# A fused hybrid decoder layer in fp32: the scores move ahead of the values in each block's run

## The chip, the cores and the metric

One core of one Trainium2 chip runs the whole kernel. The metric is device time in microseconds (us): the median of three runs. The profiler records one execution, from which the span and every duration below come.

## The reference, cut to what matters

One layer of a hybrid decoder over 4096 prompt tokens and 64 sample tokens, width 1024. All of it is float32.

```python
h = rmsnorm(x, g_pre);  z = h @ w_in          # columns: conv group, q, k, v, gates, memory q, memory gate
out_a = silu(cg) * cb * conv3(cc * ch)        # 256 channels
out_b = silu(ag) * window_attention(q, k, v)  # window 128, 8 q heads on 2 kv heads, head 64, one sink logit per head
out_c = silu(mg) * memory_attention(mq, mk, mv)   # 4 heads, 256 memory tokens
y = concat(out_a, out_b, out_c) @ w_out
x + rmsnorm(y, g_post)
```

The window attention is computed for blocks of 128 queries against 256 keys (their own block and the one before). The outputs are y for prompt and sample tokens, and the new key, value and convolution states.

## The kernel before, in words

**Two parts.** `input_projection` computes z for all tokens in three phases and leaves queries, keys, values and the gates (`mix`, group outputs that are still without attention) in memory. It ends at about 950 us. The attention part follows: 31 prompt blocks of 128 tokens, then the 64 sample tokens, then the last prompt block. The change is in the attention part alone.

**A block of the attention part.** `Block.run` multiplies the mixed operand of block b by `w_out`. The product has two halves of 512 columns, `y_0` (p = 0) and `y_1` (p = 1), each of 24 matmuls: 8 steps k of three, because fp32 is split into a rounded high part and a rest (`mh`, `ml` of the operand, and two parts of the weights). `y_0` accumulates in PSUM bank 0, `y_1` in bank 5. Each half is multiplied by the gain (DVE, `yn`) and squared and summed in place (ACT, L1466). Then DVE and POOL make the norm factor (`yst`), and DVE adds the residual (`xr`, L1476).

**The work of other blocks between the matmuls.** `events_of(i)` hangs work onto places (p, k) of block i. At (0, 0) stands `values_and_scores(i)`, at (1, 0) `transposes(i)`, at (1, 3) the split of the next block's operand (`Block.split`: ACT casts the high part `mh`, DVE subtracts for `ml`), and loads stand at others. Work on one group of 128 queries is spread over four blocks: its scores in block g - 3, the transposes of the probabilities in block g - 2, the values in block g - 1, and the output product in block g.

**The run.** `values_and_scores` issues the small matmuls that use part of the PE array (`tiled`: half the rows or half the columns at a time). They are called a block's run here. Before the change it holds, in this order: 16 matmuls of the memory values (`cross_values`, tile `pv`), then on DVE the memory gate (L1218), 16 matmuls of the window values into the same `pv`, on DVE the window gate (L1250), 12 window scores into banks 0 and 1 (`ws`), 12 memory scores into banks 4 and 5 (`xs`), and 12 window scores into banks 2 and 3. ACT copies each window score bank (L1141), and DVE puts the other half of the keys in by a predicated copy from the bank (L1142), which frees it. Softmax follows: for the memory `xmx`, `xnm`, `xp`, `xrd`, and for the window `wmx`, `wnm`, `wes`, eight exponentials on `sm` (L1153), `wden`, `wrd` and the scaling of `sm` (L1156).

**Banks.** Tags of the pool `psb` are banks 0 to 5; `pv` is a tile of two banks of its own. Bank 0 is used by `ws_0` in the run and by `y_0` after it. Bank 5 is used by `y_1` and then by `xs_1` in the next run. The transposes use banks 1 to 4.

**What sets the order.** On each engine instructions are executed in order. The order is chosen by a scheduler from dependencies and priorities at build time; `tc.keep_in_program_order(ins)` pins an instruction to its place in the program. Inside a run all tiled matmuls but the first are pinned (`run_open`). The cast `mh` is not pinned before the change. In the built program it stands on ACT directly behind the square of `y_1` and ahead of the four copies of scores, and `ml` stands on DVE ahead of the four predicated copies.

Of the kernel before, what the change touches and what calls it, by code (L numbers as in the profile page):

```python
# [15 lines left out]
P = 128  # L16
# [9 lines left out]
CT = 256  # L26
NCH = 4096 // CT
# [24 lines left out]
def hybrid_layer(ctx: ExitStack, tc: tile.TileContext, a: dict):  # L52
# [927 lines left out]
    chunks = {}  # L980

    def open_attention():
# [5 lines left out]

        ps = {tag: ctx.enter_context(tc.tile_pool(name=f"ps{tag}", bufs=1, space=bass.MemoryType.PSUM)) for tag in ("b", "pv")}
        vp = ctx.enter_context(tc.tile_pool(name="vp", bufs=5, side="right"))  # L990
# [40 lines left out]
    class Chunk:  # L1031
# [38 lines left out]
        def values(self, vt_prev, pv=None):  # L1070

            self.vts = [vt_prev]
            ts = [psum(0, f"vtp{self.c}_{i}")[:, 0:P] if pv is None else pv[:, 1, 256 + P * i : 256 + P * i + P] for i in range(2)]
            for i in range(2):
# [9 lines left out]
    class Group:  # L1084
# [24 lines left out]
        def scores(self):  # L1109
            self.open_scores(0)  # L1110
            self.open_scores(3)
            bands = [psum(n, f"ws{self.b}_{n}").rearrange("p (h k) -> p h k", h=2) for n in range(4)]
            cross = [psum(4 + hh, f"xs{self.b}_{hh}").rearrange("p (j k) -> p j k", j=2) for hh in range(2)]
            self.bands(bands[:2], 0)
            self.crosses(cross)
            self.bands(bands[2:], 1)
            self.band_softmax()

# [92 lines left out]
        def cross_values(self, o):  # L1211
            c = self.chunk
            for j in range(2):
                both_values(o[:, j * P : j * P + P], *([(third["mv"][:, kt, j * P : (j + 1) * P],
                                                         self.xpt[hh][:, CT * kt + P * j : CT * kt + P * j + P]) for kt in range(2)]
                                                       for hh in range(2)))
            g = c.mix[:, 2:4, self.i * P : self.i * P + P]
            V.tensor_tensor(g, g, o.rearrange("p (j n) -> p j n", j=2), op=ALU.mult)  # L1218

        def early_values(self, n):  # L1220
            c = self.chunk
            if n == 3:
                self.cross_values(psum(0, f"xo{self.b}")[:, :CT])
                return
# [6 lines left out]
        def values(self):  # L1231
# [11 lines left out]
            for n in range(2):  # L1243
                for kvh in range(2):
                    cs, rs = slice(64 * kvh, 64 * kvh + 64), slice(64 - 64 * n, 128 - 64 * n)
                    v, p3 = step(n, kvh)
                    tiled(o[cs, 1 - n], v[rs, cs], p3[rs, :, 64 - 64 * n : 128 - 64 * n], start=False, stop=True,
                          tile_position=(64 - 64 * n, 64 * kvh))
            g = c.mix[:, 4:8, self.i * P : self.i * P + P].rearrange("p h (a q) -> p a h q", a=2)
            V.tensor_tensor(g, g, o, op=ALU.mult)  # L1250
# [3 lines left out]
    def values_and_scores(i):  # L1254

        run_open[0] = False
        if 2 <= i + 1 < 2 * NCH:
            groups.pop(i + 1).values()
        if i + 3 < 2 * NCH:
            groups[i + 3] = Group(chunks[(i + 3) // 2], (i + 3) % 2)  # L1260
            groups[i + 3].scores()

    def transposes(i):
        g, c = i + 2, (i + 2) // 2
        if g < 2 * NCH:
            if g % 2 == 0:
                chunks[c].values(chunks[c - 1].vts[2], values_psum(f"vtp{c}"))
            groups[g].transposes()
# [148 lines left out]
    class Block:  # L1417
# [10 lines left out]
        def split(self):  # L1428
# [10 lines left out]
            hi, lo = parts(f"mh{b}"), parts(f"ml{b}")  # L1439
            S.copy(hi, src)  # L1440
            V.tensor_tensor(lo, src, f(hi), op=ALU.subtract)  # L1441
            self.hl = [hi, lo]

        def run(self, last, events):
# [6 lines left out]
            for p, (c0, c1) in enumerate(parts):  # L1451
                acc = psum((0, 5, 1)[p], f"y{b}_{p}")[:, : c1 - c0]
                j, passes = 0, 3 if m == P else 2
# [42 lines left out]
    def events_of(i):  # L1496
# [5 lines left out]

        at(0, 0, values_and_scores, i)
        if i + 2 < len(blocks):
            at(0, 0, blocks[i + 2].load)
        if i % 2 == 0:
            at(0, 1, chunk_load, i // 2 + 3)
            if i // 2 + 3 < NCH:
                at(1, 2, lambda: chunks[i // 2 + 3].load_values())
            if i == 28:  # L1510
                at(0, 1, lambda: chunks[15].load_mix())
        elif (i + 3) // 2 < NCH - 1:
            at(0, 3, lambda: chunks[(i + 3) // 2].load_mix())
        at(1, 0, transposes, i)
        if i + 1 < len(blocks) and blocks[i + 1].b != 32:
            at(1, 3, blocks[i + 1].split)
        for (n, p, k), stage in sample.items():
# [118 lines left out]
```

## Time and profile before

| | |
|---|---|
| median of 3 runs | 1606.21 us (1604.33 to 1607.09) |
| the profiled execution: time, span | 1605.98 us, 1604.3 us |
| PE busy (share of the span) | 1529.8 us (95%) |
| DVE, ACT, POOL busy | 1128.4 (70%), 777.4 (48%), 324.2 us (20%) |
| attention part, from the first score to the end | 950.9 to 1604.3 us |

The page gives busy times of each engine. Matmuls of one array shape overlap in the records, so a busy PE is not an idle-free PE: what a block costs is read from the starts of its instructions. A row of the timeline gives the start, the length, engine, line, operation, tiles and count, and in brackets the idle time of the engine before it and what ended that. PEld is the loading of weights. "The chain of waits" is the list of who waited for whom.

### The profile page before, as it was taken

The numbers are of one execution on the slowest core, as the hardware profiler recorded it, in microseconds if no ns is written. First come the engines' busy times: TensorE is split into PE (matmuls) and PEld (weight loads), VectorE is DVE, ScalarE is ACT, GpSimd is POOL, SyncE is SP. The second block draws the span as 40 slices with busy tenths as digits, with TensorE's granted clock in tenths as the row PEclk, the third lists the DMA queues.
The fourth block names the chain that finished last, engine by engine and source line by source line (L and its number), as shares of the span: only waits on it lengthen the run. The fifth ranks groups of instructions, "written<-read, shape, count | busy, mean of one in ns | idle before, by whom it ended". The sixth has DMA issues, their size and how long they took to land.

```text
span 1604.3 us, 30846 instructions
## 1 busy us (share of the span) xinstructions
PE 1529.8 (95%) x11981; PEld 1399.3 (87%) x11981; DVE 1128.4 (70%) x1850; ACT 777.4 (48%) x1964; POOL 324.2 (20%) x522
## 2 busy tenths in 40 slices
PE   9999999999999999999999998888888888888998
PEld 9999999999999999999999987777777777777776
DVE  6878888898988777976667695555555555555554
ACT  6776665565222222444435464555555555555541
POOL 0322333222100000000001022333333333333320
PEclk9999999999999999999999999999999999999999
DMA  9979999877644333798557597444444444444432
GB/s 262 213 209 264 269 274 267 277 238 187 233 167 157 121 121 131 246 294 272 190 197 243 191 303 226 132 126 130 135 131 129 125 136 131 131 130 131 143 115 92
DMA packets 169735, 299.47 MB, mean 187 GB/s; under 512 B 29813, under 2 KB 99445, under 8 KB 169557
## 3 DMA queue, kind: packets, MB, share of 16 engines
q1 hardware_dynamic: 128069, 226.69, 44.5%
q0 software_dynamic: 40800, 69.76, 16.2%
q8 instruction: 94, 1.54, 0.4%
q10 hardware_dynamic: 720, 1.05, 0.2%
q14 instruction: 52, 0.43, 0.1%
HBM read 190.38 MB, written 108.05 MB: 186 GB/s over the span
## 4 chain that ended last, share of the span: by engine, by line
PE 64%; DVE 14%; issue 8%; ACT 7%; POOL 3%; DMA 3%; SPq 0%; POOLq 0%; ACTq 0%; DVEq 0%
PE c L359 47%; PE y L1458 12%; ACT sm L1153 3%; DVE xr L1476 2%; DVE ml L1441 2%; ACT mh L1440 2%; DVE sm L1142 2%; DVE wmx L1148 1%; POOL wpt L1202 1%; DVE xmx L1161 1%; POOL yst L1472 1%; PE xt L1208 1%; PE wt L1195 1%; PE mem_acc L775 1%; ACT y L1466 1%
## 5 line engine op out<-in xcount | busy, mean ns | idle before, releaser
L1458 PE MATMUL y<-wo,mh 128*128 128x512 f32 (+1 forms) x1040 | 338.9, 396 | 42.7 <-DVE sm L1142 42.7
L1458 PEld LDWEIGHTS y<-wo,mh 128*128 128x128 f32 x1040 | 195.6, 189 | 89.8 <-DVE sm L1142 48.6
L366 DVE TENSOR_TENSOR z<-c,z 128x520 f32<-128x520 f32 (+1 forms) x308 | 195.0, 646 | 95.1 <-PE c L359 94.0
L1458 PE MATMUL y<-wo,ml 128*128 128x512 f32 (+1 forms) x520 | 202.6, 390 | 0.0
L1465 DVE TENSOR_TENSOR yn<-y,gpost 128x512 f32<-128x512 f32 (+1 forms) x66 | 45.4, 687 | 177.0 <-PE y L1458 173.5
L1458 PEld LDWEIGHTS y<-wo,ml 128*128 128x128 f32 x520 | 98.7, 190 | 17.7
L1466 ACT ACTIVATE y<-y 128x512 f32<-128x512 f32 (+1 forms) x66 | 38.0, 575 | 147.8 <-DVE yn L1465 147.8
L1168 POOL TENSOR_SCALAR xp<-xp,xrd 128x256 f32<-128x256 f32 x128 | 60.8, 486 | 224.1 <-DVE wnm L1149 122.8
L1153 ACT ACTIVATE sm<-sm,wnm 128x128 f32<-128x128 f32 x256 | 99.2, 389 | 12.9 <-DVE wnm L1149 12.9
L1164 ACT ACTIVATE xp<-xs,xnm 128x256 f32<-128x256 f32 x128 | 58.9, 473 | 66.3 <-DVE xnm L1162 66.3
L1200 POOL TENSOR_SCALAR_AFFINE_SELECT wpv<-wpt 128x512 f32<-128x512 f32 x62 | 51.8, 855 | 98.7 <-ACT wpt L1196 98.7
L1017 PEld LDWEIGHTS ws<-kst,q 64*128 64x128 f32 x768 | 50.2, 187 | 12.1 <-issue 10.8
L1017 PE MATMUL ws<-kst,q 64*128 64x256 f32 x768 | 60.0, 288 | 0.4 <-DVE z L366 0.4
L1476 DVE SCALAR_TENSOR_TENSOR xr<-yn,yst,xr 128x1024 f32<-128x1024 f32 (+2 forms) x34 | 42.5, 1253 | 22.1 <-POOL yst L1472 21.3
L1017 PE MATMUL pv<-wpv,vt 128*64 128x256 f32 (+1 forms) x240 | 39.1, 400 | 17.2 <-DVE mix L1218 8.6
L734 POOL MEMSET negs<- 128x1 f32 x1 | 0.1, 98 | 265.2 <-PE c L359 265.2
L368 ACT COPY z<-c 128x520 f32<-128x520 f32 (+1 forms) x44 | 24.4, 554 | 55.5 <-PE c L359 52.7
L1202 POOL TENSOR_SCALAR_AFFINE_SELECT wpt<-wpt 128x512 f32<-128x512 f32 x64 | 40.6, 653 | 50.7 <-ACT wpt L1196 50.4
L1142 DVE COPY_PREDICATED sm<-wmask,ws 128x256 f32<-128x256 uint8 x124 | 49.9, 441 | 0.0
L1472 POOL TENSOR_TENSOR yst<-yst,mhalf 128x1 f32<-128x1 f32 (+1 forms) x33 | 18.4, 557 | 148.0 <-DVE yst L1471 148.0
L1153 ACT ACTIVATION_READ_ACCUMULATOR sm<-sm,wnm 128x1 f32 x256 | 47.9, 187 | 0.0
L400 ACT CAST zh<-z 128x520 fp32r<-128x520 f32 x56 | 33.4, 624 | 29.2 <-DVE z L366 26.5
(957 smaller groups left out, 5027.8 us busy)
## 6 DMA issues: line engine op xcount, KB each, us to landing
q<-qd POOLq DMA_DIRECT2D x32, 768.0 KB, 8.3
xr<-in_x_p SPq DMA_DIRECT2D x32, 512.0 KB
nat<-in_x_p SPq DMA_DIRECT2D x39, 416.0 KB
o_yp<-xr SPq DMA_DIRECT2D x31, 512.0 KB
md<-th POOLq DMA_DIRECT2D x48, 260.0 KB, 6.6
qd<-zh SPq DMA_DIRECT2D x48, 260.0 KB
qd<-z SPq DMA_DIRECT2D x48, 260.0 KB
place<-md SPq DMA_DIRECT2D x8, 1024.0 KB
```

The source lines that it names most:

```text
L359: TE.matmul(bank[:, :HW], l, r, start=first and i == 0, stop=last and i == 3 * KH - 1)
L366: add = lambda dst, other: V.tensor_tensor(dst, c, other, op=ALU.add)
L1017: ins = TE.matmul(o, w, x, **kw)
L1142: V.copy_predicated(to, third["wmask"], third["negs"].unsqueeze(2).to_broadcast([P, 2, P]) if self.b == 0 else s3[:, :, 0:P])
L1153: S.activation(sm[:, h, :], sm[:, h, :], AF.Exp, bias=nm[:, h : h + 1], scale=SCALE, accum_out=den[:, h : h + 1])
L1164: S.activation(p[:, i, :], s[:, i, :], AF.Exp, bias=nm[:, i : i + 1], scale=SCALE, accum_out=den[:, i : i + 1])
L1168: G.tensor_scalar(p[:, i, :], p[:, i, :], rd[:, i : i + 1], 0.5, op0=ALU.mult, op1=ALU.mult)
L1200: G.affine_select(self.pv[u].rearrange("p (h q) -> p h q", h=4), p3, pattern=[[0, 4], [-1, P]], compare_op=ALU.is_gt, fill=0.0, base=0, ch ...
L1202: G.affine_select(p3, p3, pattern=[[0, 4], [1, P]], compare_op=ALU.is_ge, fill=0.0, base=0, channel_multiplier=-1)
L1458: TE.matmul(acc, self.hl[l][:, k], wo[k][c0 // 512][:, r, c0 % 512 : c0 % 512 + c1 - c0], start=j == 0, stop=j == passes * KT - 1)
L1466: S.activation((psum(2, "sq") if end else acc)[:m, : c1 - c0], acc[:m], AF.Square, scale=float(D) ** -0.5, accum_out=st[:m, p : p + 1])
L1476: V.scalar_tensor_tensor(self.xr[:m, cs], yn[:m, cs], st[:m, 3:4], self.xr[:m, cs], op0=ALU.mult, op1=ALU.add)
```

## The change

It reorders a block's run. The scores of group i + 3 come first, all 24 window scores before the 12 memory scores, then both values of group i + 1, and then both gates, memory and window, one behind the other (`cross_gate` is taken out of `cross_values` and called behind the window values). `band_softmax` is called after the values. The cast `mh` of blocks 1 to 30 is pinned to its place in the program, at (1, 3) of the block before. In block 0 the run is moved to (0, 3), the transposes to (1, 2) and the split to (1, 4); its two output halves use the two banks of a `pv` tile in place of banks 0 and 5, and the transposed values of chunk 1 use bank 0. The loads of values move from (1, 2) to (1, 3), and the order in which the two PSUM pools are opened is swapped.

In the built program after the change, ACT has per block: square of `y_1`, four copies of scores, two exponentials `xp` for each half, the eight of `sm`, (in every other block two copies of transposed values,) the copies of transposed probabilities with the square of `y_0` among them, and last the cast `mh`. DVE has: `yn` of `y_1`, `yst`, the predicated copy of bank 0, `xr`, the three other predicated copies, both `xmx`, `xnm`, `wmx`, `xrd`, `xnm`, `wnm`, the two gates, `xrd`, `wes`, `wden`, `wrd`, the scaling of `sm`, `yn` of `y_0`, `xpt`, and `ml`.

```diff
--- before.py
+++ after.py
@@ -986,7 +986,7 @@
         psa.close()
         pa.close()
 
-        ps = {tag: ctx.enter_context(tc.tile_pool(name=f"ps{tag}", bufs=1, space=bass.MemoryType.PSUM)) for tag in ("b", "pv")}
+        ps = {tag: ctx.enter_context(tc.tile_pool(name=f"ps{tag}", bufs=1, space=bass.MemoryType.PSUM)) for tag in ("pv", "b")}
         vp = ctx.enter_context(tc.tile_pool(name="vp", bufs=5, side="right"))
         yp = ctx.enter_context(tc.tile_pool(name="yp", bufs=2, side="right"))
         bq = att.enter_context(tc.tile_pool(name="bq", bufs=1))
@@ -1070,7 +1070,7 @@
         def values(self, vt_prev, pv=None):
 
             self.vts = [vt_prev]
-            ts = [psum(0, f"vtp{self.c}_{i}")[:, 0:P] if pv is None else pv[:, 1, 256 + P * i : 256 + P * i + P] for i in range(2)]
+            ts = [psum(0, f"vtp{self.c}_{i}")[:, 0:P] if pv is None else pv[:, P * i : P * i + P] for i in range(2)]
             for i in range(2):
                 TE.transpose(ts[i], self.vT[:, i * P : i * P + P], ident)
             for i in range(2):
@@ -1112,9 +1112,8 @@
             bands = [psum(n, f"ws{self.b}_{n}").rearrange("p (h k) -> p h k", h=2) for n in range(4)]
             cross = [psum(4 + hh, f"xs{self.b}_{hh}").rearrange("p (j k) -> p j k", j=2) for hh in range(2)]
             self.bands(bands[:2], 0)
+            self.bands(bands[2:], 1)
             self.crosses(cross)
-            self.bands(bands[2:], 1)
-            self.band_softmax()
 
         def both_rows(self, outs, q, k):
 
@@ -1214,13 +1213,17 @@
                 both_values(o[:, j * P : j * P + P], *([(third["mv"][:, kt, j * P : (j + 1) * P],
                                                          self.xpt[hh][:, CT * kt + P * j : CT * kt + P * j + P]) for kt in range(2)]
                                                        for hh in range(2)))
-            g = c.mix[:, 2:4, self.i * P : self.i * P + P]
+
+        def cross_gate(self, o):
+            g = self.chunk.mix[:, 2:4, self.i * P : self.i * P + P]
             V.tensor_tensor(g, g, o.rearrange("p (j n) -> p j n", j=2), op=ALU.mult)
 
         def early_values(self, n):
             c = self.chunk
             if n == 3:
-                self.cross_values(psum(0, f"xo{self.b}")[:, :CT])
+                o = psum(0, f"xo{self.b}")[:, :CT]
+                self.cross_values(o)
+                self.cross_gate(o)
                 return
             o = psum(0, f"wo{self.b}")
             both_values(o, *([(v, p[u]) for v, p in zip(c.vts[self.i : self.i + 2], (self.pv, self.pt)) if p[u] is not None]
@@ -1246,6 +1249,7 @@
                     v, p3 = step(n, kvh)
                     tiled(o[cs, 1 - n], v[rs, cs], p3[rs, :, 64 - 64 * n : 128 - 64 * n], start=False, stop=True,
                           tile_position=(64 - 64 * n, 64 * kvh))
+            self.cross_gate(pv[:, 0, 256 : 256 + CT])
             g = c.mix[:, 4:8, self.i * P : self.i * P + P].rearrange("p h (a q) -> p a h q", a=2)
             V.tensor_tensor(g, g, o, op=ALU.mult)
 
@@ -1253,18 +1257,21 @@
 
     def values_and_scores(i):
 
-        run_open[0] = False
+        run_open[0] = i == 0
+        g = i + 3
+        if g < 2 * NCH:
+            groups[g] = Group(chunks[g // 2], g % 2)
+            groups[g].scores()
         if 2 <= i + 1 < 2 * NCH:
             groups.pop(i + 1).values()
-        if i + 3 < 2 * NCH:
-            groups[i + 3] = Group(chunks[(i + 3) // 2], (i + 3) % 2)
-            groups[i + 3].scores()
+        if g < 2 * NCH:
+            groups[g].band_softmax()
 
     def transposes(i):
         g, c = i + 2, (i + 2) // 2
         if g < 2 * NCH:
             if g % 2 == 0:
-                chunks[c].values(chunks[c - 1].vts[2], values_psum(f"vtp{c}"))
+                chunks[c].values(chunks[c - 1].vts[2], psum(0, "vtp1")[:, :CT] if c == 1 else values_psum(f"vtp{c}")[:, 1, 256:])
             groups[g].transposes()
 
     def chunk_load(c):
@@ -1437,7 +1444,9 @@
                 return
             src = chunks[b // 2].mix[:, :, (b % 2) * P : (b % 2) * P + P]
             hi, lo = parts(f"mh{b}"), parts(f"ml{b}")
-            S.copy(hi, src)
+            copy = S.copy(hi, src)
+            if 0 < b < 31:
+                tc.keep_in_program_order(copy)
             V.tensor_tensor(lo, src, f(hi), op=ALU.subtract)
             self.hl = [hi, lo]
 
@@ -1449,7 +1458,11 @@
 
             parts = [(0, 512), (512, 768), (768, D)] if last else [(0, 512), (512, D)]
             for p, (c0, c1) in enumerate(parts):
-                acc = psum((0, 5, 1)[p], f"y{b}_{p}")[:, : c1 - c0]
+                if b == 0:
+                    both = values_psum("y0") if p == 0 else both
+                    acc = both[:, p]
+                else:
+                    acc = psum((0, 5, 1)[p], f"y{b}_{p}")[:, : c1 - c0]
                 j, passes = 0, 3 if m == P else 2
                 for k in range(KT):
                     for fn in events.get((min(p, 1), k), ()) if p < 2 else ():
@@ -1500,20 +1513,20 @@
         def at(p, k, fn, *args):
             ev.setdefault((p, k), []).append(lambda: fn(*args))
 
-        at(0, 0, values_and_scores, i)
+        at(0, 0 if i else 3, values_and_scores, i)
         if i + 2 < len(blocks):
             at(0, 0, blocks[i + 2].load)
         if i % 2 == 0:
-            at(0, 1, chunk_load, i // 2 + 3)
+            at(0, 1 if i else 4, chunk_load, i // 2 + 3)
             if i // 2 + 3 < NCH:
-                at(1, 2, lambda: chunks[i // 2 + 3].load_values())
+                at(1, 3, lambda: chunks[i // 2 + 3].load_values())
             if i == 28:
                 at(0, 1, lambda: chunks[15].load_mix())
         elif (i + 3) // 2 < NCH - 1:
             at(0, 3, lambda: chunks[(i + 3) // 2].load_mix())
-        at(1, 0, transposes, i)
+        at(1, 0 if i else 2, transposes, i)
         if i + 1 < len(blocks) and blocks[i + 1].b != 32:
-            at(1, 3, blocks[i + 1].split)
+            at(1, 3 if i else 4, blocks[i + 1].split)
         for (n, p, k), stage in sample.items():
             if n == i:
                 at(p, k, next, stage, None)
```

## The prediction

> **What bounds the kernel now.** I read the page first, for the share of the engines, then the waits of PE in the attention part, then the timeline of one pair of blocks.
>
> ```profile
> span 1604.3 us, 30846 instructions
> PE 1529.8 (95%) x11981; PEld 1399.3 (87%) x11981; DVE 1128.4 (70%) x1850; ACT 777.4 (48%) x1964; POOL 324.2 (20%) x522
> ```
>
> PE is the bound, so what counts is the time in which PE stands still. The chain of waits for PE from 956 to 1545 us has three rows (engine and tile that waited, for whom, us in total, times, longest):
>
> ```profile
> PE y L1458 <- DVE sm L1142: 42.7, 29, 3.3
> PE pv L1017 <- DVE mix L1218: 8.6, 14, 0.6
> PE pv L1017 <- DVE place L1218: 8.6, 14, 0.6
> ```
>
> There are two waits per block, in 28 blocks: one inside the run, where the window values wait for the memory gate (14 + 14 times 0.61 us), and one behind it, where `y_0` waits until bank 0 has been copied out of the scores (28 times about 1.4, and once 3.3 in block 0). The timeline of PE for one block and the next one's start:
>
> ```profile
> 1201.14 0.50 PE L1458 MATMUL y<-wo,mh 128*128 128x512 f32 x1 [1.39 <-DVE sm L1142]
> 1206.72 0.38 PE L1075 MATMUL vtp<-ident,vT 128*128 128x128 f32 x2
> 1208.60 0.47 PE L1458 MATMUL y<-wo,mh 128*128 128x512 f32 x1
> ...
> 1214.26 1.09 PE L1017 MATMUL pv<-xpt,mv 128*64 128x128 f32 x16
> 1215.97 0.65 PE L1017 MATMUL pv<-wpv,vt 128*64 128x256 f32 x4 [0.61 <-DVE mix L1218]
> ...
> 1217.58 0.98 PE L1017 MATMUL ws<-kst,q 64*128 64x256 f32 x12
> 1218.38 0.89 PE L1017 MATMUL xs<-mk,q 64*128 64x256 f32 x12
> 1219.10 0.89 PE L1017 MATMUL ws<-kst,q 64*128 64x256 f32 x12
> 1221.40 0.50 PE L1458 MATMUL y<-wo,mh 128*128 128x512 f32 x1 [1.41 <-DVE sm L1142]
> 1241.40 0.50 PE L1458 MATMUL y<-wo,mh 128*128 128x512 f32 x1 [1.39 <-DVE sm L1142]
> ```
>
> Two blocks take 1241.40 - 1201.14 = 40.26, so a block takes 20.13 us. Its run lasts from 1214.26 to 1221.40, 7.14 us. Why bank 0 comes free so late is seen on the other engines:
>
> ```profile
> 1214.37 0.69 DVE L1465 TENSOR_TENSOR yn<-y,gpost 128x512 f32<-128x512 f32 x1 [3.79 <-PE y L1458]
> 1215.15 0.58 ACT L1466 ACTIVATE y<-y 128x512 f32<-128x512 f32 x1 [4.52 <-DVE yn L1465]
> 1215.88 0.21 DVE L1471 TENSOR_SCALAR yst<-yst 128x1 f32<-128x1 f32 x1
> ...
> 1216.78 1.28 DVE L1476 SCALAR_TENSOR_TENSOR xr<-yn,yst,xr 128x1024 f32<-128x1024 f32 x1 [0.69 <-POOL yst L1472]
> 1217.98 0.68 DVE L1250 TENSOR_TENSOR mix<-mix,pv 128x512 f32<-128x512 f32 x1
> ...
> 1218.69 1.05 ACT L1440 CAST mh<-mix 128x1024 fp32r<-128x1024 f32 x1 [2.85 <-DVE mix L1250]
> ...
> 1219.65 1.19 ACT L1141 COPY sm<-ws 128x256 f32<-128x256 f32 x4
> 1219.77 1.22 DVE L1441 TENSOR_TENSOR ml<-mix,mh 128x1024 fp32r<-128x1024 f32 x1 [1.11 <-ACT mh L1440]
> 1220.92 0.77 DVE L1142 COPY_PREDICATED sm<-wmask,ws 128x256 f32<-128x256 uint8 x2
> ```
>
> It is a chain of DVE and ACT: `xr`, window gate, cast `mh`, then the copy of bank 0 behind the cast and the predicated copy behind `ml`. The scores are the last thing in the run, so nothing on PE covers it.
>
> **The run in its new order.** Its matmuls are the same, so I rebuild it from the starts above. Twelve scores take 0.80 from the first matmul to the next group (1217.58 to 1218.38) and 0.72 where the shape did not change before them (1218.38 to 1219.10); the next group of one shape thus begins 0.17 before the last one's end (1218.38 + 0.89 against 1219.10). Where the array's shape changes, the next group begins about as the last ends. So: window scores 0.80 + 0.72; memory scores 0.89, as the shape changes behind them; memory values 1.09 - 0.17 = 0.92; window values, up to the next change of shape, 1217.58 - 1215.97 = 1.61. The sum is 4.94 against 7.14: 2.20 less. There are four changes of shape before and after, so none is added. A block would take 17.93 us by PE alone.
>
> **What is late next: bank 5.** `xs_1` writes the bank of `y_1`, which is free when ACT has squared it. That is at 1215.84 (the `yst` row starts right behind it), 1.58 behind the run's start. The memory scores begin 0.80 + 0.72 = 1.52 behind it. That costs 0.1 us per block with the release, while `yn` is on time. So 18.03.
>
> **What is late next: the loop through DVE and ACT.** `ml` stands on DVE right ahead of `yn` of `y_1`, and `mh` at the end of ACT's block. A late softmax thus delays `yn`, so bank 5, so PE. The rest of the durations:
>
> ```profile
> 1201.31 1.28 DVE L1161 TENSOR_REDUCE xmx<-xs 128x2 f32<-128x512 f32 x2
> 1202.70 0.47 ACT L1164 ACTIVATE xp<-xs,xnm 128x256 f32<-128x256 f32 x1 [2.14 <-DVE xnm L1162]
> 1203.45 1.22 DVE L1148 TENSOR_REDUCE wmx<-sm 128x8 f32<-128x1024 f32 x1
> 1204.93 0.40 ACT L1153 ACTIVATE sm<-sm,wnm 128x128 f32<-128x128 f32 x1 [0.30 <-DVE wnm L1149]
> 1208.09 0.19 ACT L1153 ACTIVATION_READ_ACCUMULATOR sm<-sm,wnm 128x1 f32 x1
> 1208.75 1.23 DVE L1156 TENSOR_TENSOR sm<-sm,wrd 128x1024 f32<-128x1024 f32 x1
> 1209.10 1.05 ACT L1196 COPY wpt<-wt 128x512 f32<-128x512 f32 x2
> 1210.04 0.59 ACT L1209 COPY xpt<-xt 128x512 f32<-128x512 f32 x1
> ```
>
> From the start of `yn` (0): `yst` at 1.51, `xr` at 2.41 (1216.78 - 1214.37), its end 3.61 as the next instruction sees it (1217.98). Three predicated copies of 0.385 (0.77 for two): 4.77. Both `xmx`: 6.05. `wmx`: 7.27. The second half's exponentials can start at about 7.6, behind the small steps, and take two of 0.47: 8.5. The eight of `sm` with theirs take 1208.28 - 1204.93 = 3.35: 11.9. To the scaling 0.47 (1208.28 to 1208.75), the scaling 1.23: 13.6. `yn` of `y_0` 0.69, the square 0.6: 14.9. In every other block one copy `wpt` (0.53) comes behind the square: 15.4. `xpt` 0.59, `mh` 1.05, `ml` 1.22: 18.3, and 17.8 in the others. PE needs 18.03. So the loop and PE are nearly equal: 18.3 in one block and 18.03 in the next give 18.17 on average. I take 18.1, since each of the loop's small steps was rounded up. The two gates lie in this loop between `wnm` and `wes`, which ACT needs as its second step of the eight. They take no more than 0.68 each and end by 9.0, about when that step comes, if the values are done by 7.4; by the run above they end at 5.0. If not, what they are late is paid in the loop.
>
> The saving is 20.13 - 18.1 = 2.03 in each of 28 blocks, 56.8 us. `mh` costs nothing where it is put, since its reader comes after the next run, 5 us later.
>
> **Blocks 29 and 30** have values without scores:
>
> ```profile
> 1539.55 1.09 PE L1017 MATMUL pv<-xpt,mv 128*64 128x128 f32 x16
> ...
> 1541.47 0.65 PE L1017 MATMUL pv<-wpv,vt 128*64 128x256 f32 x4
> ```
>
> Here the window values come 1.92 behind the memory values where 0.92 would do. With the gates behind both, 1.0 goes, in two blocks 2.0. Against that, blocks 26 to 30 also carry the sample tokens' softmax on DVE and ACT, which lengthens a loop without slack: I take 1.0 back (bounds 0 and 3).
>
> **Block 0.** Here the order changes most:
>
> ```profile
> 953.49 1.23 DVE L1441 TENSOR_TENSOR ml<-place,mh 128x1024 fp32r<-128x1024 f32 x1
> 956.95 0.79 PE L1458 MATMUL y<-wo,mh 128*128 128x512 f32 x1 [3.28 <-DVE sm L1142]
> 965.12 1.04 PE L1195 MATMUL wt<-ident,sm 128*128 128x128 f32 x8
> ```
>
> ```profile
> 956.00:958.00 2.00, 1.05 (x3) 0.86 (x4) 2.00 (x5) 0.14 (x1) 0.94 (x2) 0.50 0.81 145
> 960.00:962.00 2.00, 2.00 (x6) 1.52 (x6) 1.83 (x5) 0.45 (x2) 1.48 (x4) 0.50 1.31 373
> ```
>
> `y_0` could start before the run, but its second matmul needs `ml`, which DVE ends at 954.72 behind the splits of `w_out`. So PE stands still there instead: `y_0` goes on at 954.8, 2.2 us earlier than before, but the run of 36 scores now comes into it, 2.3 to 2.5 us. The windows (PE clock is the eighth number) show that the clock granted after the gap of 3.28 us was 0.50 from 956 to 962. With a gap of about 3 us again, that stays. At half clock the run's longer stretch costs up to 3 us, at full clock the transposes come 2.2 earlier: between -2.2 and +0.8, I take -0.5. [...]
>
> The loads hang on the same queues: POOL issues `kst` and `q` right behind the scores, which now end 3 us earlier in the run, and three blocks ahead of use. I cost them at nothing; the cover is over 50 us. In block 0 they come some 8 us later, which with that cover is nothing too.
>
> **Sum.** 1605.98 - 56.8 - 2.0 + 1.0 - 0.5 = 1547.7, so **1548**. The profiled execution is 0.2 below the median, so I make no correction. A difference of 0.2% (3 us) is about what a measurement of this kernel can tell from no change.
>
> **The rivals.** (1) *The loop becomes the bound* (chance 0.22). It was computed within 0.3 of PE's need, from some 25 instructions with their handovers. If each handover costs 0.04 more, it is 1 us longer: 19.3 and 18.8, so a saving of 1.08 in 28 blocks, 30 us: 1575. In between 1557 to 1575. For it: DVE and ACT alternate without slack. Against it: the pieces are measured with their handovers. (2) *The change does not do what it says* (0.03): the predicated copy of bank 0 is still late and only the wait inside the run goes, 28 times 0.78 and 2.0: 1582. Against it: in the built order this copy stands right behind `yst`. (3) *Slower* (0.04): the exponentials no longer overlap their accumulator reads. Now the eight and one small one take 3.35 us, because the next starts 0.1 behind a read's start; without that overlap each of twelve per block costs 0.19 more, 2.3 us in the loop: 20.6 and 20.1, 20.35 on average, 0.2 over today's block: 28 times 0.2 is 6 us, 1612. It decides from a loop of 20.13 on. Against it: the rows show the overlap in the same sequence of instructions. (4) *PE alone is the bound and the start comes at full clock* (0.08): 28 times 2.2, 2.0 and 2.2: 1540.
>
> **How the numbers follow.** The forecast (0.62) spans 1542 to 1557, by 18.03 to 18.35 per block, the start, and the sample blocks. To hold 8 in 10 the range takes in half of rival 1 and some of rival 4: 1541 to 1568. Faster by over 0.2% is the forecast and rivals 1, 2 and 4: 0.95, within 0.2% 0.01, slower 0.04.
>
> **What would show it right or wrong.** In the profile after, the row of `pv` waiting for the memory gate should be gone, and that of `y` waiting for `sm` should be left in block 0 at most. A block should take 18.0 to 18.3 us. A new wait of `xs` for ACT's square of `y_1`, with 0.1 to 0.3 us, should appear. If it is 0.5 or more, rival 1 holds; its sign is `ml` ending behind the last matmul of `y_1`. If `y` still waits for `sm` by a microsecond, rival 2 does. The prediction is wrong if the blocks take over 18.8 us.

## The result, and the profile after

The changed kernel takes 1550.01 us (median of 4 runs, 1548.36 to 1553.61) against 1606.03 us (4 runs of the kernel before): a ratio of 0.9655, 95% interval 0.9635 to 0.9675. The prediction, 1548.0 with a range of 1541 to 1568, was right. The profiled execution took 1549.02 us, 56.96 less than the one before.

Three lines of the page after: the span, the engines' busy times, and the chain that ended last, which before the change began with PE 64%, DVE 14%.

```profile
span 1547.3 us, 30906 instructions
PE 1525.7 (99%) x11981; PEld 1400.8 (91%) x11981; DVE 1124.6 (73%) x1850; ACT 776.8 (50%) x1964; POOL 335.6 (22%) x522
...
PE 88%; DVE 4%; issue 3%; DMA 2%; ACT 2%; POOL 1%; SPq 0%; DVEq 0%; POOLq 0%; ACTq 0%
```

PE, DVE and ACT are busy about as long as before; PE no longer stands still. All waits of PE from 956 to 1545 us in the kernel after (for whom, us in total, times, longest):

```profile
PE y L1471 <- ACT y L1479: 3.3, 1, 3.3
PE xt L1207 <- ACT sq L1320: 0.3, 1, 0.3
```

Both waits per block are gone, and the one row of any size that is left is a single wait, in block 0 (two earlier ones of block 0 lie ahead of 956 us and are told below). The timeline of one block after, PE's rows of the run with those of DVE and ACT that release it:

```profile
1178.40 0.50 PE L1471 MATMUL y<-wo,mh 128*128 128x512 f32 x1
...
1190.15 1.23 DVE L1450 TENSOR_TENSOR ml<-place,mh 128x1024 fp32r<-128x1024 f32 x1 [2.13 <-ACT mh L1447]
...
1191.54 1.69 PE L1017 MATMUL ws<-kst,q 64*128 64x256 f32 x24
1191.64 0.69 DVE L1478 TENSOR_TENSOR yn<-y,gpost 128x512 f32<-128x512 f32 x1 [0.27 <-PE y L1471]
1192.43 0.58 ACT L1479 ACTIVATE y<-y 128x512 f32<-128x512 f32 x1 [2.31 <-DVE yn L1478]
...
1193.07 1.07 PE L1017 MATMUL xs<-mk,q 64*128 64x256 f32 x12
...
1193.41 0.45 DVE L1141 COPY_PREDICATED sm<-wmask,ws 128x256 f32<-128x256 uint8 x1
...
1194.07 1.09 PE L1017 MATMUL pv<-xpt,mv 128*64 128x128 f32 x16
1194.99 0.60 PE L1017 MATMUL pv<-wpv,vt 128*64 128x256 f32 x4
...
1196.55 0.50 PE L1471 MATMUL y<-wo,mh 128*128 128x512 f32 x1
...
1214.44 0.50 PE L1471 MATMUL y<-wo,mh 128*128 128x512 f32 x1
```

Two blocks take 1214.44 - 1178.40 = 36.04, so a block takes 18.02 us (20.13 before). The run lasts 1196.55 - 1191.54 = 5.01 us (7.14 before). The predicated copy of bank 0 ends at 1193.86, 2.7 us before `y_0` wants the bank. Before the change this copy was the last thing that `y_0` waited for.

Where the 57.0 us between the two spans come from, by the starts of the runs in both traces:

| stretch | before | after | difference |
|---|---|---|---|
| start to run 1 | 972.41 | 975.25 | +2.84 |
| run 1 to run 29 (28 blocks) | 567.14 | 508.08 | -59.06 |
| run 29 to the end | 64.75 | 63.97 | -0.78 |

The loop gave 2.11 per block, a little more than forecast, and block 0 lost what was not forecast.

### The profile page after: what moved, and what is told of

Its sections match the earlier page's. It is cut to its first block, busy times and chain, and to the rows that moved or that the text cites. A ratio compares the mean times of both kernels' runs of the same rounds, so it can differ in the third digit from the quotient of the medians.

```text
span 1547.3 us, 30906 instructions
## 1 busy us (share of the span) xinstructions
PE 1525.7 (99%) x11981; PEld 1400.8 (91%) x11981; DVE 1124.6 (73%) x1850; ACT 776.8 (50%) x1964; POOL 335.6 (22%) x522
## 4 chain that ended last, share of the span: by engine, by line
PE 88%; DVE 4%; issue 3%; DMA 2%; ACT 2%; POOL 1%; SPq 0%; DVEq 0%; POOLq 0%; ACTq 0%
PE c L359 49%; PE y L1471 24%; PE pv L1017 5%; PE ws L1017 3%; PE xt L1207 2%; PE xs L1017 2%; PE wt L1194 2%; PE mem_acc L775 1%; DMA wor<-in_w_out 1%; ACT sm L1152 1%; DMA vd<-v 1%; DVE z L366 0%; DMA wr_2A<-in_w_in 0%; DVE wo L182 0%; POOL md L163 0%
## 5 line engine op out<-in xcount | busy, mean ns | idle before, releaser
L1199 POOL TENSOR_SCALAR_AFFINE_SELECT wpv<-wpt 128x512 f32<-128x512 f32 x62 | 62.4, 1018 | 115.5 <-ACT wpt L1195 109.8
L1153 DVE TENSOR_TENSOR wden<-wden,wes 128x8 f32<-128x8 f32 x32 | 5.3, 167 | 88.3 <-ACT sm L1152 88.3
L1017 PE MATMUL ws<-kst,q 64*128 64x256 f32 x768 | 55.4, 290 | 0.0
```

The costliest lines, as they stand in the source:

```text
L1017: ins = TE.matmul(o, w, x, **kw)
L1199: G.affine_select(self.pv[u].rearrange("p (h q) -> p h q", h=4), p3, pattern=[[0, 4], [-1, P]], compare_op=ALU.is_gt, fill=0.0, base=0, ch ...
```

## The experiments

The kernel before ran beside each group of experiments, on other chips, with medians of 1607 to 1611 us. So the ratios are compared. "Block" is the mean distance between the starts of two runs over the same 21 blocks of each trace, 20.15 for the kernel before and 18.02 for the one after.

### One part of the change at a time

**The pinned cast alone**, on the kernel before:

```diff
-            S.copy(hi, src)
+            copy = S.copy(hi, src)
+            if 0 < b < 31:
+                tc.keep_in_program_order(copy)
```

> The kernel before with one part of the change alone: the cast `mh` is pinned to (1, 3) of the block before. The scores stay last in the run, the memory gate stays between the values. Theory A (the chain of DVE and ACT behind `yn` held bank 0, and the whole loop from `yn` to the next `yn` is nearly as long as a block): the wait of `y` for bank 0 goes (28 times 1.4 = 39 us, to 1567), but the scores of banks 2 and 3 now end some 5.6 us behind `yn` instead of 2.4, and the window gate stands ahead of the predicated copies, so the softmax ends about 1 us later; the loop is 18.3 + 1.0 and 17.8 + 1.0 and becomes the bound at about 19.05 a block: 1606 - 28 x 1.1 = 1575 (1567 to 1585). Rival B (only the order of the scores frees bank 0 in time): about 1606. Rival C (the loop has room): 1567, the wait for the memory gate of 0.61 stays and no other appears.

Measured: ratio 0.9755 (0.9720 to 0.9791), 1568.15 us, block 18.68. The waits of PE from 980 to 1500 us in this kernel:

```profile
PE pv L1017 <- DVE place L1218: 8.8, 14, 0.8
PE pv L1017 <- DVE mix L1218: 8.0, 13, 0.6
```

The wait for bank 0 is gone from the loop and the wait for the memory gate stays. That is rival C, 1567: the loop through DVE and ACT had room, and theory A's extra microsecond did not come. The sum of the prediction has the scaling of `sm` ahead of ACT's copies; in this timeline it lies beside them (the scaling starts at 1192.91, the copies of transposed values at 1192.94).

**The gates alone**, on the kernel before (no pin, scores last):

```diff
-            g = c.mix[:, 2:4, self.i * P : self.i * P + P]
+        def cross_gate(self, o):
+            g = self.chunk.mix[:, 2:4, self.i * P : self.i * P + P]
             V.tensor_tensor(g, g, o.rearrange("p (j n) -> p j n", j=2), op=ALU.mult)
...
+            self.cross_gate(pv[:, 0, 256 : 256 + CT])
             g = c.mix[:, 4:8, self.i * P : self.i * P + P].rearrange("p h (a q) -> p a h q", a=2)
```

> The kernel before with one part of the change alone: the memory gate stands behind the window values, ahead of the window gate; the scores stay last, the cast is not pinned. Theory A (a block before is set by one chain of DVE and ACT from the end of `y_1` over `yn`, `yst`, `xr`, window gate, `mh`, `ml` to the copy of bank 0, and the wait inside the run lies beside this chain): the wait inside the run goes and the wait of `y` grows by as much and by the memory gate's 0.35 on top, as this gate now stands on the chain: 20.13 + 0.35 a block, 1606 + 10 - 2 (blocks 29 and 30) = 1614, with a `y` wait of about 2.5 us. Rival B (the two waits add up, as a sum over waits says): 28 x 0.78 + 2 less, 1582, with a `y` wait of 1.4 us as before.

Measured: ratio 1.0196 (1.0146 to 1.0247), 1640.52 us. One of the two waits was removed, and the kernel became slower. The waits of PE from 990 to 1560 us in this kernel:

```profile
PE y L1463 <- DVE sm L1142: 71.4, 27, 2.9
```

The wait of `y` grew from 1.4 to 2.62 in most blocks, as theory A had it: the two waits lay on one chain. But blocks are of two kinds in this trace. Twelve have the expected length (20.40 and 20.64 in turn, 0.37 over the kernel before, 0.35 expected). In fifteen PE is slow after the wait and the block takes about 22.1 (two of them, which also carry work of the sample tokens, take longer). Here are two stretches of 3 us behind a wait of 2.62, with the start of `y` in each, from the same trace (in the windows the third number is PE's busy time and the eighth the granted clock):

```profile
1171.90:1174.90 3.00, 3.00 (x13) 2.46 (x14) 2.96 (x8) 1.44 (x7) 0.15 (x1) 1.00 1.20 380
1214.84:1217.84 3.00, 3.00 (x7) 2.42 (x8) 2.96 (x8) 1.43 (x7) 0.16 (x1) 0.50 1.18 359
```

```profile
1171.90 0.50 PE L1463 MATMUL y<-wo,mh 128*128 128x512 f32 x1 [2.62 <-DVE sm L1142]
...
1214.84 0.79 PE L1463 MATMUL y<-wo,mh 128*128 128x512 f32 x1 [2.62 <-DVE sm L1142]
```

At the same wait one stretch is granted 1.00 and the other 0.50. Fifteen blocks times 1.6 us, and 28 times 0.37, make 34 us, about what the ratio gives (0.0196 of 1606 is 31). Theory A was right on the chain and blind to this.

**The pin and the gates together**, scores still last, block 0 as before (both diffs above):

> The kernel before with the pinned cast and both gates behind both values; the scores stay last in the run, block 0 is as before. Theory A (the scores have to come first so that the softmax, and with it the loop through DVE and ACT, starts early): PE alone would need 17.9 a block, but both gates stand ahead of the predicated copies, so the loop is 18.3 + 1.4 and 17.8 + 1.4: about 19.4 a block, 1606 - 28 x 0.7 - 2 = 1584 (1570 to 1592). Rival B (the order of scores and values does not matter once both waits are gone): 18.0 a block and no loss in block 0, 1544 to 1550.

Measured: ratio 0.9743 (0.9711 to 0.9775), 1566.39 us, block 18.70. That is below theory A's range and far from rival B: both missed. The wait of PE in this kernel from 980 to 1500 us, and DVE's rows ahead of `y_0` in one block:

```profile
PE y L1465 <- DVE sm L1142: 21.3, 27, 1.0
```

```profile
1218.33 1.28 DVE L1483 SCALAR_TENSOR_TENSOR xr<-yn,yst,xr 128x1024 f32<-128x1024 f32 x1 [0.67 <-POOL yst L1479]
1219.53 0.41 DVE L1220 TENSOR_TENSOR mix<-mix,pv 128x256 f32<-128x256 f32 x1
...
1219.86 0.68 DVE L1255 TENSOR_TENSOR mix<-mix,pv 128x512 f32<-128x512 f32 x1
...
1220.46 0.77 DVE L1142 COPY_PREDICATED sm<-wmask,ws 128x256 f32<-128x256 uint8 x2
...
1220.94 0.50 PE L1465 MATMUL y<-wo,mh 128*128 128x512 f32 x1 [0.62 <-DVE sm L1142]
```

The wait for bank 0 is back, 21.3 / 27 = 0.79 per block, in place of the 0.62 inside the run. With the scores last, `xr` and both gates stand ahead of the copy that frees bank 0. With the cast out of the way, moving the gate only moves the wait, and the two kernels have the same block within 0.02. The last 0.68 per block (18.70 to 18.02, 19 us) needs the scores at the front of the run. What they bring with the memory gate still between the values was not run.

**The changed kernel without the pin:**

```diff
-            copy = S.copy(hi, src)
-            if 0 < b < 31:
-                tc.keep_in_program_order(copy)
+            S.copy(hi, src)
```

> The changed kernel without the pinned cast. In the built program `mh` then stands on ACT behind the eight exponentials and ahead of the copies of the transposed probabilities, and `ml` on DVE between `yn` of `y_0` and `xpt`. Theory A (bank 0 is copied out early in any case, and PE is the bound): 1548 to 1551, and the loop is shorter by up to one `ml` (1.2 us), so that `ml` no longer stands ahead of `yn`. Rival B (the copies of the transposed probabilities, 1.05 later, hold PE or the square of `y_0`): 0.5 a block or more, 1564 and over.

Measured: ratio 0.9649 (0.9617 to 0.9680), 1551.80 us, block 18.02: theory A. In the new order the pin is worth nothing that shows here. It also shows who the bound is. DVE's row at the end of a block in this kernel:

```profile
1192.28 0.69 DVE L1476 TENSOR_TENSOR yn<-y,gpost 128x512 f32<-128x512 f32 x1 [2.37 <-PE y L1469]
```

DVE now waits 2.37 us for PE ahead of `yn`, against 0.27 in the changed kernel's block above, and the block has the same length. PE is the bound.

### How near the next limits are

**The memory scores between the window scores**, in the changed kernel:

```diff
             self.bands(bands[:2], 0)
-            self.bands(bands[2:], 1)
             self.crosses(cross)
+            self.bands(bands[2:], 1)
```

> The changed kernel with the memory scores between the two halves of the window scores, in the order that they had before. Theory A (in the changed kernel the memory scores start 1.53 behind the run's start, and bank 5 is free at 1.57: the second place of 12 window scores is just the cover that the square of `y_1` needs): `xs` starts at 0.80 and waits 0.75 per block, 28 times, 21 us: 1571, with a row of `xs` waiting for ACT's square. Rival B (the wait is taken from a reserve elsewhere, as the block is bound by DVE and ACT): 1550 to 1555.

Measured: ratio 0.9803 (0.9774 to 0.9832), 1574.68 us, block 18.74, 0.72 more: theory A. From this kernel's trace, `xs` around its wait:

```profile
1195.79 0.28 PE L1017 MATMUL xs<-mk,q 64*128 64x256 f32 x1
1195.86 0.58 ACT L1479 ACTIVATE y<-y 128x512 f32<-128x512 f32 x1 [3.00 <-DVE yn L1478]
1196.60 0.98 PE L1017 MATMUL xs<-mk,q 64*128 64x256 f32 x11 [0.54 <-ACT y L1479]
```

`xs_1` goes on 0.74 behind the start of the square (1195.86 to 1196.60). With the square at 1192.43, as in the timeline of the changed kernel above, that is 1193.17, and there `xs` begins at 1193.07: bank 5 comes free just in time. Twelve more scores ahead of it are all the cover that there is.

**A longer loop**, in the changed kernel (ACT repeats one copy, so no part of the result changes):

```diff
-            (S.copy if u else V.tensor_copy)(self.xpt[u], t)
+            for _ in range(3 if u and ps is not None else 1):
+                (S.copy if u else V.tensor_copy)(self.xpt[u], t)
```

> The changed kernel, where ACT does its copy `xpt_1` of each block three times (0.59 us each, so 1.18 more, between the square of `y_0` and the cast `mh`; the same data). It lengthens the loop through ACT and DVE without touching PE. Theory A (PE is the bound, the loop lies 0.25 below it in one block and 0.47 in the next, which is the idle time of DVE ahead of `yn`): 1.18 - 0.36 = 0.82 more per block, 18.83 on average, 28 x 0.82 = 23 us: 1573, with `ml` ending behind the last matmul of `y_1` and a new wait of `xs` of about 0.8. Rival B (the loop is the bound already): 28 x 1.18 = 33 us, 1583. Rival C (ACT has room before `mh`, so the loop doesn't run through it): 1550.

Measured: ratio 0.9775 (0.9748 to 0.9802), 1571.37 us, block 18.75, 0.73 more, where 0.82 was expected: theory A. Its trace at the end of a block:

```profile
1197.56 1.84 ACT L1209 COPY xpt<-xt 128x512 f32<-128x512 f32 x3
1199.30 1.05 ACT L1448 CAST mh<-place 128x1024 fp32r<-128x1024 f32 x1
1200.38 1.23 DVE L1451 TENSOR_TENSOR ml<-place,mh 128x1024 fp32r<-128x1024 f32 x1 [3.37 <-ACT mh L1448]
...
1201.52 0.68 DVE L1479 TENSOR_TENSOR yn<-y,gpost 128x512 f32<-128x512 f32 x1
...
1202.98 0.98 PE L1017 MATMUL xs<-mk,q 64*128 64x256 f32 x11 [0.65 <-ACT y L1480]
```

This is how rival 1 of the prediction would have looked: `yn` has no idle time ahead of it, it follows `ml`, and `xs` waits 0.65. From one `yn` of `y_1` to the next this trace has 18.98 and 18.52 in turn. The three copies take 1.84, and the one in the changed kernel 0.60; without the 1.24 the loop is 17.74 and 17.28, 17.5 on average, about 0.5 under PE's 18.02.

### Block 0

Rows of block 0 in the changed kernel, from the last matmul of the input projection to the start of run 1:

```profile
948.51 0.28 PE L359 MATMUL c<-hi_7T,w_2A 128*128 128x260 f32 x1
...
953.32 0.50 PE L1471 MATMUL y<-wo,ml 128*128 128x512 f32 x1 [2.73 <-DVE ml L1450]
...
956.34 2.22 PE L1017 MATMUL ws<-kst,q 64*128 64x256 f32 x24
...
967.39 0.59 ACT L1479 ACTIVATE y<-y 128x512 f32<-128x512 f32 x1
...
968.15 0.79 PE L1471 MATMUL y<-wo,mh 128*128 128x512 f32 x1 [3.25 <-ACT y L1479]
...
975.25 1.69 PE L1017 MATMUL ws<-kst,q 64*128 64x256 f32 x24
```

There are two long gaps, and one was not forecast: `y_1` waits 3.25 us for ACT's square of `y_0`. (A third, of 1.30 us, stands ahead of `y_0`, for the cast `mh`.) Both halves are one tile, and ACT does the square behind the eight exponentials. The windows of this trace show the clock after each gap:

```profile
954.00:958.00 4.00, 4.00 (x25) 3.02 (x25) 1.09 (x2) 0.11 (x1) 0.81 (x2) 0.57 0.91 197
...
966.00:970.00 4.00, 1.85 (x4) 1.49 (x5) 1.59 (x3) 4.00 (x16) 1.04 (x2) 0.73 1.23 345
970.00:974.00 4.00, 4.00 (x16) 3.25 (x15) 1.69 (x1) 0.79 (x1) 1.44 (x3) 0.85 1.16 382
```

The trace also keeps each stretch of granted clock with its start and length. By these records PE runs at half clock (granted 0.50) no longer than before the change: 6.83 us in one stretch before (from 955.68), two stretches of 3.41 us after (from 954.15 and from 967.81). Most of block 0's loss is the standing still, 1.30 + 2.73 + 3.25 = 7.28 us against 0.36 + 3.28 = 3.64 before.

**Block 0's `y_1` in bank 5:**

```diff
-                    both = values_psum("y0") if p == 0 else both
-                    acc = both[:, p]
+                    acc = values_psum("y0")[:, 0] if p == 0 else psum(5, "y0_1")
```

> The changed kernel, where block 0's `y_1` uses bank 5 in place of the second bank of the tile that `y_0` is in. Theory A (block 0's 3.25 us wait of `y_1` is there because both halves are one tile, so that `y_1` waits for ACT's square of `y_0` behind the eight exponentials; the gap then halves the clock for about 3 us more): `y_1` starts behind the transposes, at about 964.9 on the profile's clock instead of 968.15, at full clock, 3.3 + 1.1 = 4.4 us earlier; then `ml` of block 1, which ends at 972.5 and stands ahead of `yn` of `y_1` on DVE, holds bank 5, and the next run's `xs` waits about 1.5 us for it: net 3, 1547 (1545.5 to 1548). Rival B (something else on ACT or DVE holds block 1 back as long, so the gap only moves): 1550, and run 1 starts no earlier than 26.4 us behind the input projection.

Measured: ratio 0.9637 (0.9608 to 0.9665), 1548.42 us.

**Block 0 in its old order**, in the changed kernel (excerpt; the other places go back likewise, the transposed values to the tile of the values):

```diff
-        run_open[0] = i == 0
+        run_open[0] = False
...
-                if b == 0:
-                    both = values_psum("y0") if p == 0 else both
-                    acc = both[:, p]
-                else:
-                    acc = psum((0, 5, 1)[p], f"y{b}_{p}")[:, : c1 - c0]
+                acc = psum((0, 5, 1)[p], f"y{b}_{p}")[:, : c1 - c0]
...
-        at(0, 0 if i else 3, values_and_scores, i)
+        at(0, 0, values_and_scores, i)
...
-        at(1, 0 if i else 2, transposes, i)
+        at(1, 0, transposes, i)
```

> The changed kernel with block 0 as it was before the change: the run at (0, 0) ahead of `y_0`, the transposes at (1, 0), the split at (1, 3), `y_0` and `y_1` in banks 0 and 5. The order inside the runs, the gates and the pinned cast stay. Theory A (block 0 lost time by its new place of the run: 26.46 us from the end of the input projection to the start of run 1, against 21.88 before): with the scores first, bank 0 is copied earlier than before, `y_0` starts about 955.2 - 950.5 = 4.7 behind the input projection instead of 6.4, and the gap on PE of about 1.7 in place of 3.28 leaves the clock at full: run 1 starts 18.5 to 21 behind the input projection: 1542 to 1545. Rival B (the gap of 3.28 stays, as `ml` and the splits of the weights hold DVE): 21.9, 1545.5. Rival C (block 0's old order is no better under the new order of the run): 1550.

Measured: ratio 0.9620 (0.9593 to 0.9647), 1546.79 us.

**The old order with `y_0` in the values' banks** (the diff just above, but `y_0` and `y_1` as in the kernel with `y_1` in bank 5, and the transposed values of chunk 1 in bank 0), and **the same with the pools in the old order**:

```diff
-for tag in ("pv", "b")}
+for tag in ("b", "pv")}
```

> Block 0 in its old order, as in the kernel with the old block 0 (run ahead of `y_0`, transposes at (1, 0), split at (1, 3)), but `y_0` in the tile of the values' banks, so that it need not wait until bank 0 is copied, `y_1` in bank 5, and the transposed values of chunk 1 in bank 0. Theory A (block 0 is set by the gaps of PE, of which the old order has 2.1 for the scores and 2.1 for bank 0): the second gap goes, run 1 starts 18 to 19 behind the end of the input projection instead of 20.3, and run 3 at 56.5 to 58 instead of 58.6: 1545 (1543.5 to 1547). Rival B (DVE and ACT, on which the softmax, `ml` and the splits of `w_out` stand, set it): run 3 at 58.6, equal to the kernel with the old block 0, 1547.

> The kernel before this one with the two PSUM pools opened in the order of the kernel before the change. Theory A (the swapped pools place `ws_0` in a bank whose last use in the input projection is late, hence the wait of 2.1 of the scores for DVE's sum, against 0.36 before): the scores start 0.4 behind the input projection instead of 2.3, and run 3 starts up to 2 us earlier, 54.5 to 57 behind it: 1543.5 (1541.5 to 1546). Rival B (DVE and ACT set it): equal to the previous kernel within 0.5 us by the start of run 3.

Measured: 0.9634 (0.9608 to 0.9660), 1550.51 us, and 0.9678 (0.9653 to 0.9703), 1555.63 us.

The changed kernel once more on that chip:

> The changed kernel as it is, once more, on the chip of the two kernels that follow. Every theory: 0.9655 of the kernel before (0.9635 to 0.9675), 1548 to 1553.

Measured: 0.9634 (0.9610 to 0.9657), 1549.81 us.

The totals do not separate these kernels: the intervals overlap, and the end of the input projection, which none of them touches, lies between 947.4 and 955.0 us in their traces. Counted from that end, the traces do:

| kernel | input ends | run 1 behind it | run 3 behind it | end behind it |
|---|---|---|---|---|
| before | 950.53 | 21.88 | (other loop) | (other loop) |
| after, two profiles | 948.79, 947.37 | 26.46, 26.15 | 62.32, 62.03 | 598.5, 598.4 |
| `y_1` in bank 5 | 948.82 | 21.75 | 58.98 | 595.3 |
| old block 0 | 951.93 | 20.27 | 58.57 | 594.9 |
| old order, `y_0` in the values' banks | 954.97 | 19.10 | 57.47 | 593.8 |
| the same, pools in the old order | 953.71 | 19.98 | 61.85 | 598.2 |

Rows of `y_1`'s start and of the next `xs` in the kernel with `y_1` in bank 5, then of the scores' and `y_0`'s start in the one with the old block 0, then of run 1's start in the last two kernels, and the window around it in the last one:

```profile
963.78 0.50 PE L1470 MATMUL y<-wo,mh 128*128 128x512 f32 x1 [0.57 <-ACT xp L1163]
...
973.38 0.98 PE L1017 MATMUL xs<-mk,q 64*128 64x256 f32 x11 [1.00 <-ACT y L1478]
```

```profile
954.25 1.70 PE L1017 MATMUL ws<-kst,q 64*128 64x256 f32 x24 [2.10 <-DVE z L366]
...
958.77 0.50 PE L1467 MATMUL y<-wo,mh 128*128 128x512 f32 x1 [2.10 <-DVE sm L1141]
```

```profile
974.07 1.69 PE L1017 MATMUL ws<-kst,q 64*128 64x256 f32 x24 [1.89 <-ACT xpt L1208]
```

```profile
973.69 3.40 PE L1017 MATMUL ws<-kst,q 64*128 64x256 f32 x24 [3.30 <-ACT vt L1081]
```

```profile
973.15:983.39 10.24, 7.60 (x58) 6.52 (x60) 7.74 (x14) 4.63 (x14) 3.06 (x5) 0.50 1.23 369
```

With bank 5, `y_1` starts after 0.57 in place of 3.25, and 1.00 of the gain goes back to `xs` in the next run: 3.2 us net (62.2 to 59.0), where theory A said 3. Run 1 is back at 21.75, where it was before the change (21.88). So the shared tile is shown as the cause of block 0's loss. The old block 0 gains 3.6, with two gaps of 2.10 and no slow matmuls behind them: the 24 scores take 1.70 and the first `y` 0.50. It was expected with one gap only: here the scores wait for DVE's last sums too. In the kernel after that, `y_0`'s wait goes and 1.1 more is gained, as theory A had it by the trace (57.47 by run 3; run 1's 19.10 is 0.1 over its range), though a wait of 1.89 for ACT's copy comes in run 1; its total is no better, as its input projection ended at 954.97. With the pools in the old order the scores do start about 1.9 us earlier behind the input's end (953.64 against 956.85), as theory A had it. But run 1's wait is then 3.30, for the copies of the transposed values in bank 0, and behind it PE runs at half clock for 10.24 us, as the window shows (0.50): the 24 scores take 3.40 in place of 1.69. That loses the gain, and theory A missed it.

By run 3 the best of these are 3 to 5 us ahead of the changed kernel, and they still are at the end (last column). By total time none is shown to beat it, since that is what the ends of the input projection scatter by. Why these ends differ between kernels stays open.

## Why the prediction was right, step by step

- **The run, 7.14 to 4.94:** 5.01 measured, 1196.55 - 1191.54. Its parts: 1.53 to `xs` (1.52), 1.00 to the memory values (0.89), 0.92 (0.92), 1.56 to `y_0` (1.61). The 0.11 over in the second is the step that was put down to bank 5.
- **Bank 5, 0.1 per block:** the size was right, the sign that was named was not. No wait of `xs` appears as a row. The group of twelve takes 1.07 in place of 0.88 to 0.89, and the kernel with the memory scores second shows what the cover is worth.
- **The loop, 18.3 and 17.8:** each too long by 0.5; 17.74 and 17.28 by the kernel with the longer loop. The sum took whole rows, while the next instruction starts about 0.1 before the end that a row shows: in the rows of that kernel, 1197.56 + 1.84 = 1199.40 against `mh` at 1199.30, and 1200.38 + 1.23 = 1201.61 against `yn` at 1201.52. The forecast took 18.1 as the compromise between loop and PE, and PE's 18.03 alone was right (18.02). The alternation that the trace has, 17.89 and 18.15, was there before (20.02 and 20.26) and goes with the two transposes of values that every other block has on PE. So the saving was 2.11 in 28 blocks, 59.06 us with the sample's part in blocks 27 and 28, and not 56.8. Rival 1 was a real one: 0.5 us away, and its sign is seen where the loop was lengthened.
- **Blocks 29 and 30, -2.0 + 1.0:** -0.78 from run 29 to the end. That the sum of the two came close is luck, since both were wrong. The 1.92 us from the memory values to the window values were read as a wait, but in the kernel before three matmuls of `y` stand in them:

```profile
1540.58 0.50 PE L1458 MATMUL y<-wo,mh 128*128 128x512 f32 x1
1540.91 0.40 PE L1458 MATMUL y<-wo,ml 128*128 128x512 f32 x1
1541.15 0.39 PE L1458 MATMUL y<-wo,mh 128*128 128x512 f32 x1
```

  After the change the window values come 0.93 and 0.92 behind the memory values, as forecast, but those matmuls have to follow later. From run 29 to run 30 only 0.35 is saved (22.51 to 22.16), and about 0.4 from there to the end. So the gates brought about 0.4 per block in place of 1.0, and nothing is left that the sample's softmax took back here.
- **`mh` costs nothing where it is put:** yes, and in the new order nothing also where it is not pinned.
- **Block 0, -0.5 (-2.2 to +0.8):** this step failed. From the end of the input projection to run 1 block 0 lost 4.6 us (21.88 to 26.46); 1.7 of that came back by an earlier end of the input. The prediction saw `y_0`'s new gap (2.73 for `ml`, "about 3" forecast) and left the second out: it did not ask who frees the tile when `y_0` and `y_1` are put into one. After it the clock fell a second time, to 0.73 and 0.85 in the windows that follow, where the prediction counted one slow stretch; the two together are as long as the one before the change.
- **The sum:** 2.26 too little in the loop, 0.22 too much at the end, and 3.34 too little loss in block 0. The forecast of 1547.7 was 1.3 under the profiled execution because two misses took each other away. So its closeness is luck in part; the range and the mechanism of the loop did not need that luck.
- **The other rivals:** rival 2, that the change would not do what it says, was wrong, as no `y` waits for `sm`. The exponentials still overlap their accumulator reads (from 1200.80 to 1202.82 in the changed kernel's trace, each of `sm` starts 0.09 to 0.10 behind the start of the read ahead of it), so nothing became slower. The loop went as in rival 4, "PE alone", but for the 0.1 of bank 5 (18.02 per block), and the start came without its full clock (0.57, 0.73 and 0.85 in the windows of block 0).

What the prediction did not see is how the parts of the change hang together. The pin alone brings 39 us (0.0245 of 1606), the gates alone cost time, pin and gates together bring no more than the pin, and with the scores in front the pin is no longer needed. A table of waits adds up the idle time but not what its removal brings: the wait inside the run and the one behind it were two places of one chain.

## What to carry to other kernels

Before a wait is counted as a gain, follow the chain that releases the next wait behind it: if it starts ahead of both, removing the first only lengthens the second. What helps is to put the producer of a late-freed buffer where other work covers it, and then to ask for every buffer that was merged or moved who reads it last and what stands ahead of that reader. And judge a start-up variant by times within the trace, from an event that none of the variants touches, where the totals scatter by more than its worth.

## What the runs showed of the hardware that was not expected

The granted clock fell around gaps of PE that are below 3 us, and not around each. In the kernel with the gates alone, 27 blocks had a gap of 2.6 to 2.9 us, 25 of them within 0.02 of 2.63; in 15 of the blocks matmuls behind it ran at half clock for a while, in 12 all at full clock. The mean clock granted in that execution is 0.981, and 0.996 in the profiled one of the kernel before. Of its two stretches of 3 us in the section on the experiments, each behind a wait of 2.62, one is granted 1.00 and the other 0.50. So the length of the gap alone did not decide it there; what did is not shown.

The other traces, by the gap of PE and the clock granted:

- The kernel before, in the loop: gaps of 1.4 to 1.5 us, and 1.00 all the way from 962.51 to 1600.80 us.
- The kernel with the old block 0: two gaps of 2.10; behind them the 24 scores take 1.70 and the first `y` 0.50, about as in the stretches granted 1.00.
- Block 0 of the changed kernel: gaps of 2.73 and 3.25, and 0.50 for 3.41 us from 954.15 and again from 967.81.
- Block 0 of the kernel before: a gap of 3.28, and 0.50 for 6.83 us from 955.68.
- Run 1 with the pools in the old order: a gap of 3.30, and 0.50 for 10.24 us from 973.15.

By an estimate from the changed kernel's stretches, 3.41 us at half clock cost up to half of that, 1.7 us, near the 1.6 by which the fifteen blocks are longer.
